# First feed-forward layer of a hybrid block: activations stationary in its first products, and the residual's affine part on VectorE

## The chip, the cores and the metric

The kernel runs on one core of one Trainium2 chip. The metric is device time in microseconds (us), the median of several executions. In the views, PE is TensorE (PEld its weight loads), DVE is VectorE, ACT is ScalarE, POOL is GpSimd and SP is SyncE, whose queue issues all the DMAs.

## What is computed

One block of a model on 256 tokens of width 2048, in fp32, batch 1: a feed-forward layer, a mixer (differential attention and a gated delta rule), and a second feed-forward layer, each with an affine modulation from a vector c and with a residual and a layer norm behind it.

```python
ada = (silu(c) @ w_ada + b_ada).reshape(B, 3, 3, D)
shift, scale, gate = ada[:, :, 0, None], ada[:, :, 1, None], ada[:, :, 2, None]
y = swiglu_ffn(x * (1.0 + scale[:, 0]) + shift[:, 0], w_ffn_in[0], w_ffn_out[0])
x = layer_norm(ALPHA * x + 0.5 * gate[:, 0] * y, ln_g[0], ln_b[0])
y = hybrid_mixer(x * (1.0 + scale[:, 1]) + shift[:, 1], ...)
x = layer_norm(ALPHA * x + gate[:, 1] * y, ln_g[1], ln_b[1])
y = swiglu_ffn(x * (1.0 + scale[:, 2]) + shift[:, 2], w_ffn_in[1], w_ffn_out[1])
x = layer_norm(ALPHA * x + 0.5 * gate[:, 2] * y, ln_g[2], ln_b[2])
```

`swiglu_ffn(h, w_in, w_out)` is `(silu(g) * u) @ w_out` with `g, u` the two halves of `h @ w_in`; each half is 5632 wide, 44 tiles of 128.

## The kernel before

**Products in three parts.** Every fp32 operand of a large product is split into a high half (`hi`, rounded to fp32r by ScalarE) and a low half (`lo`, the difference, by VectorE or GpSimd), and `mm3` makes a product of three matmuls: hi by hi, and the two mixed ones. There are two forms. With *weights stationary* (`_products`) a 128x128 piece of the weights stays in the array and 256 columns of the activations (all tokens) stream past it; the result has features on partitions. With *activations stationary* (`_xprod`, `_xstat`) a tile of 128 tokens stays and 512 columns of weights stream; the result has tokens on partitions, and to be the next layer's input it has to be turned by transposes (the `hT` tiles).

**The weight stream.** `k.plan` lists all weight chunks of 128 x 1024 (512 KB) in the order of use. `_dma` issues chunk `i` on SP's queue into one of 6 `raw` buffers, `_split` makes `hi` and `lo` of it in one of 4 pairs of buffers, and `weights()` hands a chunk to the products while up to three more are split ahead. `pool_lo` says who makes `lo`: GpSimd for every chunk (1), for every second one (2), or VectorE always (0).

**The order of work.** All engines run in order. The order is written by the program itself while it is built: the products are emitted in a straight line, with a planned clock `k.t` that they advance, and side jobs are generators ("threads") that `pump()` resumes between products when their planned time has come. `yield 8.0` in such a job means: not before 8 planned us from now. `bank()` hands out 4 PSUM banks in turn and `k.read` names the job that empties one.

**The first layer.** Its input h is made tile by tile (16 tiles of 128 features, `_first_h`): four chunks `sar` of w_ada per tile are loaded, VectorE reduces each to one column, then scales the tile of x (`hf`), ScalarE makes `h_hi` and GpSimd `h_lo`. Since h comes slowly, `start` visits the first 28 pairs of (gate, up) feature tiles several times, each time with the few tiles of h that are there. `VISITS` holds (first tile of h, number of tiles, pairs from, to), `START_LO` the `pool_lo` of each visit. A pair's bank holds gate and up side by side; it is copied to `acc` at the first visit (ScalarE) and added to it at the others (VectorE). At the last visit `_ffn_hid` adds, applies silu (ScalarE), multiplies and splits (VectorE, ScalarE). The products are named `mms`. The other 16 pairs of this layer, and the second feed-forward layer, are made by `_ffn_block`, activations stationary, four pairs (512 features) at a time: gate into two banks (two halves of the tokens), up into two more, silu, product, eight transposes, split. The second matrix's products (`_y_blocks`) follow, named `mx` as well.

**Side work beside it.** `_Ada` makes the gate rows on VectorE: chunks `ar` are multiplied and added into `acc<-ar,cs,acc`; at each quarter's end its sum is split (`acchi`, `acclo`) and two matmuls (`aps`) stand for it in PE's queue.

**The residual's affine part.** Behind a layer norm the kernel keeps x without ln_g and ln_b. For the mixer's and the second layer's residual, `_load_x` fetches x again, and then for each of four quarters loads a row of ln_g and of ln_b to all partitions (`rowg`, `rowb`, one buffer each) and has GpSimd multiply and add, four instructions of 128x512 a quarter.

**The layer norm.** `_Next.step(0)` sets `pool_lo` to 1 ahead of a layer's last output block, `rest` sets it back, so that GpSimd makes the low halves of the weights there.

Of the kernel before, what the change touches and what calls it, by code (L numbers as in the profile page):

```python
# [91 lines left out]
class _Kernel:  # L92
# [52 lines left out]
    def mm3(self, ps, lhs, rhs, start, stop):  # L145
        mm = self.nc.tensor.matmul
        mm(ps, lhsT=lhs[0], rhs=rhs[0], start=start, stop=False, skip_group_check=True)  # L147
        mm(ps, lhsT=lhs[0], rhs=rhs[1], start=False, stop=False, skip_group_check=True)  # L148
        mm(ps, lhsT=lhs[1], rhs=rhs[0], start=False, stop=stop, skip_group_check=True)  # L149
        self.t += 3 * _cols(ps) * 4.22e-4  # L150
# [136 lines left out]
def _xprod(k, ps, w, act, kt, j, t, lo, hi, last):  # L287
# [261 lines left out]
class _Next:  # L549
# [5 lines left out]
    def step(self, stage, ada, ln):  # L555
        k = self.k
        if stage == 0:
            k.pool_lo = 1
# [14 lines left out]
    def rest(self, ln):  # L573
# [20 lines left out]
        k.pool_lo = 0  # L594
# [81 lines left out]
def _load_x(k, a, pool, rows, tags, idx, delay, pace):  # L676
# [11 lines left out]
    for q in range(4 if idx is not None else 0):  # L688
# [56 lines left out]
def _ffn_hid(k, ps, hid, j, acc=None, back=1):  # L745

    hid.job(j, k.read(_ffn_hid_run(k, ps, hid, j, acc, hid.all[-1:]), back))


def _ffn_hid_run(k, ps, hid, j, acc, before):  # L750
    u = k.uid()
    g, up = ps[:, 0, :], ps[:, 1, :]
    if acc is not None:
        yield 0.2
        k.V.tensor_tensor(acc, acc, ps, ALU.add)
        g, up = acc[:, 0, :], acc[:, 1, :]
    yield 0.2
    while not all(th.done for th in before):
        yield 0.3
    sg = k.hp.tile([128, S], F32, tag="sg", name=f"sg{u}", bufs=2)  # L760
    k.A.activation(sg, g, AF.Silu)
    yield
    hf = k.hp.tile([128, S], F32, tag="hidf", name=f"hidf{u}", bufs=2)
    k.V.tensor_tensor(hf, sg, up, ALU.mult)
    yield
    both = k.hp.tile([128, 2, S], F32R, tag=f"hid{j}", name=f"hid{u}")
    hid[0][j], hid[1][j] = both[:, 0, :], both[:, 1, :]
    k.A.activation(hid[0][j], hf, AF.Copy)
    yield
    k.V.tensor_tensor(hid[1][j], hf, hid[0][j].bitcast(F32), ALU.subtract)  # L770


def _ffn_block(k, h, hid, b, before, pre):
# [5 lines left out]
    def gate(t, ps, lo, hi):  # L779
        yield 0.2  # L780
# [3 lines left out]
        k.A.activation(sg[t], ps, AF.Silu)  # L784

    def up(t, ps, lo, hi):
        yield 0.2
        k.V.tensor_tensor(sg[t], sg[t], ps, ALU.mult)
# [21 lines left out]
    if pre is None:  # L810
        _xstat(k, KT // 2, h, gate)
    else:
        for t in range(2):
            k.read(gate(t, pre[t], 0, 512), 2 - t)
    _xstat(k, KT // 2, h, up)
# [6 lines left out]
def _ffn(k, a, h, sub, items, interval, start, pre, finish, tail):  # L822
# [3 lines left out]
    with ExitStack() as fs:  # L826
        k.hp = hp = fs.enter_context(tc.tile_pool(name=f"hid{sub}", bufs=1))
        for half, size in enumerate(SIZES[sub]):
# [20 lines left out]
            turned = []  # L849
            for b in range(b0, size // 4):  # L850
                turned = [_ffn_block(k, h, hid, b, turned, None if b or half else pre)]
# [586 lines left out]
def _first_h(k, a, h, hp):  # L1438
# [18 lines left out]
    for i in range(SRAW):  # L1457
        load()
        if i == 3:
            loadx(0)  # L1460
    loadx(2)
    due = 0.0
    for i, (f, half, kind) in enumerate(plan):
# [11 lines left out]
        if i in FIRST_LOADS:  # L1475
            k._dma()
# [14 lines left out]
def tile_hybrid_block(ctx: ExitStack, tc: tile.TileContext, names, aps):  # L1491
# [83 lines left out]
    def start(h, hid, side):  # L1575

        with ExitStack() as st:
# [5 lines left out]
            accs = [k.hp.tile([128, 2, S], F32, tag=f"hid{j}", name=f"acc{j}") for j in range(hid.ready)]  # L1583
            k.pool_lo = 1
            for (kt0, n, ja, jb), lo in zip(VISITS, START_LO):
                h.need(k, kt0)
                k.pool_lo = lo
                npair, nchunk = max(1, 4 // n), max(1, n // 4)
                last = kt0 + n == KT
                for j0 in range(ja, jb, npair):  # L1590
                    pss = [k.bank([128, 2, S], "mms") for q in range(npair)]
                    for c in range(nchunk):
                        w = [x.rearrange("p (q r) -> p q r", q=npair) for x in k.weights()]
# [3 lines left out]
                    for q, ps in enumerate(pss):  # L1597
                        j = j0 + q
                        if last:
                            _ffn_hid(k, ps, hid, j, accs[j], npair - q)  # L1600
                        else:
                            k.read(add(accs[j], ps, kt0 == 0), npair - q)
                    if last and first is not None:
                        k.wait(lambda: first.done)
                        first = None
                        _ada_keep(k)
# [158 lines left out]
```

## Time and profile before

| | |
|---|---|
| three timed runs, us | 2392.42, 2392.65, 2395.93; median 2392.65 |
| profiled execution, us | 2389.68, span 2387.9 |
| mean granted TensorE clock | 0.984 |
| busy share of the span | PE 97%, PEld 87%, DVE 71%, ACT 43%, POOL 14% |
| moved by DMA | 581.70 MB, 244 GB/s on the mean |

Matmuls overlap, and a matmul's end is modelled; so how many start in a stretch says more than PE's busy time. The `x` count in a table of stretches is that number (a few records can be missing). In a row of the waits or of the timeline, the bracket holds the idle time ahead of the instruction and what ended it.

### The profile page before, as it was taken

How to read it: one execution, taken by the hardware profiler on the slowest of the kernel's cores; microseconds unless marked ns; L12 is line 12 of the kernel's file. 1: busy time of each engine (PE TensorE's matmuls, PEld its weight loads, DVE VectorE, ACT ScalarE, POOL GpSimd, SP SyncE). 2: the span in 40 equal slices, each digit the busy share in tenths (PEclk: the TensorE clock that was granted, in tenths of full speed). 3: DMA queues.
4: the chain of work that ended last, by engine and by line, in shares of the span. 5: the costliest groups of instructions: out<-in, count | busy, mean ns of one | idle time of the engine just before them, and what ended most of it. 6: DMA issues, size and time to landing. Idle time of an engine off the chain costs nothing.

```text
span 2387.9 us, 36796 instructions
## 1 busy us (share of the span) xinstructions
PE 2305.5 (97%) x14217; PEld 2071.9 (87%) x14217; DVE 1707.0 (71%) x2508; ACT 1033.1 (43%) x1390; POOL 329.1 (14%) x218
## 2 busy tenths in 40 slices
PE   6999999999999899999999999999999999999997
PEld 6999997888888889988999999987878888888886
DVE  5667888787775688878887887786787555544556
ACT  4434444434444444454444434444444443444432
POOL 5884000000001310000000220013050000000001
PEclk8999999999999999999999999999999999999999
DMA  9998878899875566454546888876888556655553
GB/s 362 332 327 292 300 250 274 305 339 322 315 267 189 176 204 209 157 173 149 170 162 244 298 296 306 286 282 204 310 302 309 189 192 194 193 187 192 188 187 111
DMA packets 166359, 581.70 MB, mean 244 GB/s; under 512 B 19820, under 2 KB 22812, under 8 KB 165416
## 3 DMA queue, kind: packets, MB, share of 16 engines
q1 hardware_dynamic: 166184, 579.36, 70.7%
q8 instruction: 111, 1.82, 0.3%
q14 instruction: 64, 0.52, 0.1%
HBM read 572.98 MB, written 7.88 MB: 243 GB/s over the span
## 4 chain that ended last, share of the span: by engine, by line
PE 86%; DVE 7%; issue 2%; DMA 1%; POOL 1%; ACT 1%; SPq 0%; DVEq 0%; ACTq 0%; POOLq 0%
PE mx L148 17%; PE mx L147 17%; PE mx L149 17%; PE mm L147 6%; PE mm L148 6%; PE mm L149 6%; PE mms L148 4%; PE mms L149 4%; PE mms L147 4%; DVE lo L88 2%; DVE acc L88 1%; PE UY L153 1%; DVE x L88 1%; ACT hi L88 1%; PE hT L158 1%
## 5 line engine op out<-in xcount | busy, mean ns | idle before, releaser
L88 ACT ACTIVATE hi<-raw 128x1024 fp32r<-128x1024 f32 x769 | 811.6, 1059 | 968.7 <-PE mx L149 669.3
L88 DVE TENSOR_TENSOR lo<-raw,hi 128x1024 fp32r<-128x1024 f32 x690 | 855.7, 1246 | 495.7 <-ACT hi L88 485.4
L147 PE MATMUL mx<-hi,h_hi 128*128 128x512 f32 x992 | 389.7, 393 | 0.0
L149 PE MATMUL mx<-hi,h_lo 128*128 128x512 f32 x992 | 387.2, 390 | 0.0
L148 PE MATMUL mx<-lo,h_hi 128*128 128x512 f32 x992 | 387.0, 390 | 0.0
L147 PE MATMUL mm<-h_hi,hi 128*128 128x256 f32 x1216 | 354.4, 291 | 0.0
L149 PE MATMUL mm<-h_hi,lo 128*128 128x256 f32 x1216 | 346.5, 285 | 3.4 <-DVE lo L88 3.4
L148 PE MATMUL mm<-h_lo,hi 128*128 128x256 f32 x1216 | 346.4, 285 | 0.0
L88 POOL TENSOR_TENSOR lo<-raw,hi 128x1024 fp32r<-128x1024 f32 x79 | 190.2, 2415 | 788.0 <-ACT hi L88 788.0
L147 PE MATMUL mx<-hi,hid 128*128 128x512 f32 (+1 forms) x768 | 285.1, 371 | 1.4 <-ACT hi L88 1.4
L148 PE MATMUL mx<-lo,hid 128*128 128x512 f32 (+1 forms) x768 | 284.7, 371 | 0.8 <-DVE lo L88 0.8
L149 PE MATMUL mx<-hi,hid 128*128 128x512 f32 (+1 forms) x768 | 284.5, 370 | 0.0
L147 PE MATMUL mms<-h_hi,hi 128*128 128x256 f32 x896 | 256.2, 286 | 10.2 <-ACT hi L88 5.9
L148 PE MATMUL mms<-h_lo,hi 128*128 128x256 f32 x896 | 256.2, 286 | 3.7 <-POOL h_lo L88 3.7
L149 PE MATMUL mms<-h_hi,lo 128*128 128x256 f32 x896 | 255.9, 286 | 1.6 <-POOL lo L88 1.6
L149 PEld LDWEIGHTS mm<-h_hi,lo 128*128 128x128 f32 x1216 | 235.2, 193 | 3.9 <-DVE lo L88 3.9
L147 PEld LDWEIGHTS mm<-h_hi,hi 128*128 128x128 f32 x1216 | 235.7, 194 | 1.7 <-issue 1.6
L148 PEld LDWEIGHTS mm<-h_lo,hi 128*128 128x128 f32 x1216 | 235.7, 194 | 0.7 <-issue 0.6
L149 PEld LDWEIGHTS mx<-hi,h_lo 128*128 128x128 f32 x992 | 186.6, 188 | 39.2
L147 PEld LDWEIGHTS mx<-hi,h_hi 128*128 128x128 f32 x992 | 186.7, 188 | 38.2 <-issue 0.2
L148 PEld LDWEIGHTS mx<-lo,h_hi 128*128 128x128 f32 x992 | 186.7, 188 | 38.0 <-issue 0.2
L147 PEld LDWEIGHTS mms<-h_hi,hi 128*128 128x128 f32 x896 | 174.4, 195 | 10.9 <-ACT hi L88 6.1
(304 smaller groups left out, 3236.2 us busy)
## 6 DMA issues: line engine op xcount, KB each, us to landing
raw<-in_w_ffn_in_dram SPq DMA_DIRECT2D x240, 512.0 KB, 4.7
raw<-in_w_ffn_out_dram SPq DMA_DIRECT2D x176, 512.0 KB, 4.1
raw<-in_w_first_dram SPq DMA_DIRECT2D x112, 512.0 KB, 5.0
ar<-in_w_gate_dram SPq DMA_DIRECT2D x96, 512.0 KB, 5.1
ar<-in_w_ada_dram SPq DMA_DIRECT2D x96, 512.0 KB, 5.1
sar<-in_w_ada_dram SPq DMA_DIRECT2D x64, 512.0 KB, 5.0
raw<-in_w_gab_dram SPq DMA_DIRECT2D x64, 512.0 KB, 4.5
raw<-in_w_kq_dram SPq DMA_DIRECT2D x32, 512.0 KB, 3.6
```

The source lines that it names most:

```text
L88: return f(*args, **kw)
L147: mm(ps, lhsT=lhs[0], rhs=rhs[0], start=start, stop=False, skip_group_check=True)
L148: mm(ps, lhsT=lhs[0], rhs=rhs[1], start=False, stop=False, skip_group_check=True)
L149: mm(ps, lhsT=lhs[1], rhs=rhs[0], start=False, stop=stop, skip_group_check=True)
L153: self.nc.tensor.matmul(ps, lhsT=lhsT, rhs=rhs, start=start, stop=stop, skip_group_check=True)
L158: self.nc.tensor.transpose(ps, src, self.ident if ident is None else ident)
```

## The change

1. The first layer's visits make blocks of four pairs with activations stationary. `VISITS` now counts blocks of four pairs: the first two visits take one tile of h each and two blocks; the third takes tiles 0 and 1 for the other five; the others have the old ranges. With one tile, one chunk holds gate and up of a block, in four banks. With more, `_xbanks` makes gate and then up, in two banks each. The last visit ends in the same `_ffn_block` as the other blocks, which adds `acc` first. `_ffn_hid` goes.
2. `mm3` gets an order; in `_xprod` the two matmuls with the high half of the weights come first.
3. At the start two chunks of `w_first` are issued behind the first x tile instead of behind the first two reductions. The first two chunks are split while `pool_lo` is still 0, so VectorE makes their low halves.
4. `_Next` no longer sets `pool_lo`.
5. The affine part's products and sums are VectorE's, one each 2 planned us, the first 6 behind the loads.

```diff
-VISITS = ((0, 2, 0, 28), (2, 2, 0, 28), (4, 4, 0, 28), (8, 4, 0, 12), (8, 8, 12, 28), (12, 4, 0, 12))
+VISITS = ((0, 1, 0, 2), (1, 1, 0, 2), (0, 2, 2, 7), (2, 2, 0, 7), (4, 4, 0, 7), (8, 4, 0, 3), (8, 8, 3, 7), (12, 4, 0, 3))
-FIRST_LOADS = (0, 1)
-START_LO = (1, 1, 1, 2, 0, 0)
+START_LO = (1, 1, 1, 1, 1, 2, 0, 0)
...
+    def mm3(self, ps, lhs, rhs, start, stop, order=((0, 0), (0, 1), (1, 0))):
+        for n, (i, j) in enumerate(order):
+            self.nc.tensor.matmul(ps, lhsT=lhs[i], rhs=rhs[j], start=start and n == 0, stop=stop and n == 2,
+                                  skip_group_check=True)
...
-          start=(kt == 0), stop=(kt == last))
+          start=(kt == first), stop=(kt == last), order=((0, 0), (1, 0), (0, 1)))
...
+def _xbanks(k, kt0, n, act, name="mx"):
+
+    pss = [k.bank([128, 512], name) for _ in range(2)]
+    for c in range(n // 2):
+        w = k.weights()
+        for j in range(2):
+            for t in range(2):
+                _xprod(k, pss[t], w, act, kt0 + 2 * c + j, j, t, 0, 512, kt0 + n - 1, kt0)
+    return pss
...
         if stage == 0:
-            k.pool_lo = 1
...
         ln.norm(1, 0)
-        k.pool_lo = 0
...
-        yield 8.0
+        yield 4.0
         for t in range(2):
-            k.P.tensor_tensor(x[t][:, sl], x[t][:, sl], g, ALU.mult)
-            k.P.tensor_tensor(x[t][:, sl], x[t][:, sl], b, ALU.add)
+            for v, op in ((g, ALU.mult), (b, ALU.add)):
+                yield 2.0
+                k.V.tensor_tensor(x[t][:, sl], x[t][:, sl], v, op)
...
+    def summed(i, t, ps):
+        if accs is None:
+            return ps
+        acc = accs[4 * b + 2 * i + t]
+        k.V.tensor_tensor(acc, acc, ps, ALU.add)
+        return acc
...
+    for i in range(2):
+        k._dma()
     loadx(2)
...
-        if i in FIRST_LOADS:
-            k._dma()
...
+                if n == 1:
+                    for b in range(ba, bb):
+                        w = k.weights()
+                        pss = [k.bank([128, 512], "mms") for _ in range(4)]
                         for q, ps in enumerate(pss):
-                            _products(k, ps, [x[:, q, :] for x in w], kt0 + 4 * c, n // nchunk, [h, h], c == 0,
-                                      c == nchunk - 1)
+                            _xprod(k, ps, w, h, kt0, q // 2, q % 2, 0, 512, kt0, kt0)
+                        for q, ps in enumerate(pss):
+                            k.read(add(accs[4 * b + q], ps, kt0 == 0), 4 - q)
+                    continue
+                for b in range(ba, bb):
+                    if kt0 + n < KT:
+                        for i in range(2):
+                            for t, ps in enumerate(_xbanks(k, kt0, n, h, "mms")):
+                                k.read(add(accs[4 * b + 2 * i + t], ps, kt0 == 0), 2 - t)
+                        continue
...
+                    _ffn_block(k, hid, b, hid.all[-1:], banks, accs)
```

The order on PE at its first products, before (`mms` are banks, `h_hi`, `h_lo` the halves of h, `hi`, `lo` those of a weight chunk):

```order
L147 MATMUL mms_199<-h_hi_91,hi_187 128x256
L148 MATMUL mms_199<-h_lo_92,hi_187 128x256
L149 MATMUL mms_199<-h_hi_91,lo_188 128x256
L147 MATMUL mms_199<-h_hi_91,hi_187 128x256
L148 MATMUL mms_199<-h_lo_92,hi_187 128x256
```

and now, at the same place:

```order
L146 MATMUL mms_211<-hi_187,h_hi_91 128x512
L146 MATMUL mms_211<-hi_187,h_lo_92 128x512
L146 MATMUL mms_211<-lo_188,h_hi_91 128x512
L146 MATMUL mms_212<-hi_187,h_hi_91 128x512
L146 MATMUL mms_212<-hi_187,h_lo_92 128x512
```

What streams and what stays have changed places, a matmul is twice as wide, and the weights' low half comes last.

The order on PE in the last visit's first block, now (`hT` are the banks of the transposes of the block made before it, `sg` its products on VectorE):

```order
L146 MATMUL mms_2756<-hi_2691,h_hi_91 128x512
L146 MATMUL mms_2756<-hi_2691,h_lo_92 128x512
L146 MATMUL mms_2756<-lo_2692,h_hi_91 128x512
L156 MATMUL hT_2777<-ident,sg_2640 128x128
L156 MATMUL hT_2777<-ident,sg_2643 128x128
L156 MATMUL hT_2777<-ident,sg_2640 128x128
L156 MATMUL hT_2777<-ident,sg_2643 128x128
L146 MATMUL mms_2755<-hi_2711,h_hi_91 128x512
```

Before, no transposes stand in this part of PE's queue; now two groups of four stand there for each block.

The order on VectorE at the mixer's first quarter of the affine part, now (`x` two halves of the tokens, `lo` a chunk's low half, `acc<-ar` a gate step):

```order
L87 TENSOR_TENSOR x_12568<-x_12568,rowg_12987 128x512
L87 TENSOR_TENSOR lo_13103<-raw_12904,hi_13102 128x1024
L87 TENSOR_TENSOR x_12568<-x_12568,rowb_12988 128x512
L87 TENSOR_TENSOR x_12569<-x_12569,rowg_12987 128x512
L87 TENSOR_TENSOR lo_13138<-raw_12937,hi_13137 128x1024
L87 TENSOR_TENSOR x_12569<-x_12569,rowb_12988 128x512
L87 SCALAR_TENSOR_TENSOR acc_12870<-ar_13023,cs,acc_12870 128x512 x2
```

Before, the four lines with `rowg` and `rowb` stand on GpSimd, and the others follow each other on VectorE.

## Rows read from the trace of the kernel before

**Rows 1.** The page: busy time with share of the span, and the chain's shares.
```profile
PE 2305.5 (97%) x14217; PEld 2071.9 (87%) x14217; DVE 1707.0 (71%) x2508; ACT 1033.1 (43%) x1390; POOL 329.1 (14%) x218
...
PE 86%; DVE 7%; issue 2%; DMA 1%; POOL 1%; ACT 1%; SPq 0%; DVEq 0%; ACTq 0%; POOLq 0%
```
**Rows 2.** Stretches for one tile: length, busy (x instructions) by engine, clock, DMA (`mms`, `mx`).
```profile
60.00:120.00 60.00, 60.00 (x502) 59.97 (x501) 20.77 (x31) 4.27 (x8) 1.00 0.92 333
...
480.00:540.00 60.00, 60.00 (x266) 49.67 (x266) 2.74 (x4) 0.00 (x0) 1.00 0.92 332
```
**Rows 3.** Timeline of PE, transposes in the first layer's other blocks: start, length, instruction.
```profile
570.06 0.60 PE L158 MATMUL hT<-ident,sg 128*128 128x128 f32 x4
...
570.73 0.40 PE L148 MATMUL mx<-lo,h_hi 128*128 128x512 f32 x1
```
**Rows 4.** Timeline of the start, and a stretch (PE, PEld, DVE, ACT, POOL).
```profile
12.75 0.42 ACT L88 ACTIVATE h_hi<-hf 128x256 fp32r<-128x256 f32 x1 [10.19 <-DVE hf L88]
...
14.54 1.06 ACT L88 ACTIVATE hi<-raw 128x1024 fp32r<-128x1024 f32 x1 [1.37 <-DMA raw<-in_w_first_dram]
...
15.65 0.58 PE L147 MATMUL mms<-h_hi,hi 128*128 128x256 f32 x1 [5.91 <-ACT hi L88]
...
27.45 0.58 PE L148 MATMUL mms<-h_lo,hi 128*128 128x256 f32 x1 [3.25 <-POOL h_lo L88]
...
10.00:40.00 30.00, 15.15 (x93) 14.27 (x94) 18.67 (x28) 11.33 (x16) 16.76 (x9) 0.66 1.02 404
```
**Rows 5.** Two stretches at the first layer's end, and PE's timeline.
```profile
330.00:350.00 20.00, 15.59 (x106) 14.79 (x105) 17.56 (x28) 7.91 (x14) 0.00 (x0) 0.83 0.69 220
360.00:390.00 30.00, 25.99 (x114) 20.29 (x114) 25.84 (x36) 15.04 (x23) 0.00 (x0) 1.00 0.82 273
...
336.35 0.79 PE L153 MATMUL aps<-acchi,ones 128*128 128x512 f32 x1 [3.46 <-ACT acchi L88]
338.09 0.79 PE L153 MATMUL aps<-acclo,ones 128*128 128x512 f32 x1 [0.95 <-DVE acclo L88]
```
**Rows 6.** Groups of VectorE, 0 to 400 us: count, busy us, mean ns, idle before.
```profile
L88 DVE TENSOR_TENSOR lo<-raw,hi 128x1024 fp32r<-128x1024 f32 x62 | 76.6, 1236 | 35.2 <-ACT hi L88 35.1
L88 DVE TENSOR_TENSOR acc<-acc,mms 128x512 f32<-128x512 f32 x96 | 64.7, 682 | 36.2 <-PE mms L149 30.6 <-ACT acc L88 5.6
...
L88 DVE SCALAR_TENSOR_TENSOR acc<-ar,cs,acc 128x512 f32<-128x512 f32 x52 | 38.9, 749 | 1.0
...
L88 DVE TENSOR_TENSOR hidf<-sg,acc 128x256 f32<-128x256 f32 x28 | 11.7, 418 | 0.0
```
**Rows 7.** The affine part: timeline of VectorE and PE, stretches, landing of `rowg`.
```profile
1749.41 3.48 DVE L88 SCALAR_TENSOR_TENSOR acc<-ar,cs,acc 128x512 f32<-128x512 f32 x2
...
1380.72 0.79 PE L153 MATMUL aps<-acchi,ones 128*128 128x512 f32 x1 [3.03 <-ACT acchi L88]
...
1370.00:1390.00 20.00, 16.69 (x112) 15.89 (x111) 18.86 (x15) 7.00 (x9) 14.38 (x8) 0.83 0.87 295
...
1750.00:1770.00 20.00, 17.80 (x78) 14.20 (x77) 19.19 (x15) 8.55 (x11) 13.21 (x8) 1.00 0.82 270
...
DMA to landing us min/median/max: 4.7/4.7/4.7
```
**Rows 8.** Timeline of GpSimd and VectorE at the first layer norm.
```profile
782.27 2.39 POOL L88 TENSOR_TENSOR lo<-raw,hi 128x1024 fp32r<-128x1024 f32 x1 [0.48 <-ACT hi L88]
...
782.52 0.42 DVE L88 SCALAR_TENSOR_TENSOR res<-mx,gate 128x256 f32<-128x256 f32 x1 [13.59 <-PE mx L149]
782.98 1.97 DVE L88 TENSOR_TENSOR x<-x,res 128x256 f32<-128x256 f32 x1
```
**Rows 9.** Stretches of all engines: the last two columns are DMA share and GB/s.
```profile
60.00:120.00 60.00, 60.00 (x502) 59.97 (x501) 42.38 (x63) 27.41 (x33) 52.67 (x26) 1.00 0.92 333
...
40.00:50.00 10.00, 10.00 (x85) 10.00 (x85) 5.85 (x10) 6.91 (x11) 9.11 (x5) 1.00 1.02 409
```
**Rows 10.** The transposes' tile `hT`: idle time ahead of it until VectorE's product.
```profile
  DVE sg L88: 0.3, 1
```

More of the change, by code (lines that the diff above doesn't have):

```diff
@@ L284, in _tile, with _xprod @@
     return part[kt] if isinstance(part, dict) else part[:, kt, :]
-def _xprod(k, ps, w, act, kt, j, t, lo, hi, last):
+def _xprod(k, ps, w, act, kt, j, t, lo, hi, last, first=0):
     act.need(k, kt)
@@ L740, in _y_blocks, with _ffn_block, gate @@
         return finish.step(3, ada, ln)
[L745 to L753, printed above, removed]
-        yield 0.2
[L755 to L773, printed above, removed]
-    sg = {}
-    def gate(t, ps, lo, hi):
-        yield 0.2
+def _ffn_block(k, hid, b, before, banks, accs=None):
+    sg = {}
+    def summed(i, t, ps):
[4 more added lines that the diff above has]
+        return acc
+    def gate(t, ps):
+        yield 0.2
+        src = summed(0, t, ps)
         while not all(th.done for th in before):
@@ L783, in gate, with up @@
         sg[t] = k.hp.tile([128, 512], F32, tag=f"sg{t}", name=f"sg{k.uid()}")
-        k.A.activation(sg[t], ps, AF.Silu)
-    def up(t, ps, lo, hi):
+        k.A.activation(sg[t], src, AF.Silu)
+    def up(t, ps):
         yield 0.2
-        k.V.tensor_tensor(sg[t], sg[t], ps, ALU.mult)
+        src = summed(1, t, ps)
+        while t not in sg:
+            yield 0.3
+        k.V.tensor_tensor(sg[t], sg[t], src, ALU.mult)
     def turn(ups):
@@ L808, in turn @@
                 k.V.tensor_tensor(hid[1][j], ps[:, q, :], hid[0][j].bitcast(F32), ALU.subtract)
[L810 to L815, printed above, removed]
+    for i, done in enumerate((gate, up)):
+        for t, ps in enumerate(banks(i)):
+            k.read(done(t, ps), 2 - t)
     th = k.spawn(turn(list(k.users[-2:])))
@@ L848, in _ffn, with banks @@
                     ada = side()
-            turned = []
+            turned = hid.all[-1:]
             for b in range(b0, size // 4):
-                turned = [_ffn_block(k, h, hid, b, turned, None if b or half else pre)]
+                def banks(i, b=b):
+                    return pre if pre and b == half == i == 0 else _xbanks(k, 0, KT, h)
+                turned = [_ffn_block(k, hid, b, turned, banks)]
             res = _y_blocks(k, size // 2, hid, ada, sub, half == 0, ln if half else None, finish, tail)
@@ L1582, in start @@
             first.step()
-            accs = [k.hp.tile([128, 2, S], F32, tag=f"hid{j}", name=f"acc{j}") for j in range(hid.ready)]
-            k.pool_lo = 1
-            for (kt0, n, ja, jb), lo in zip(VISITS, START_LO):
+            accs = [k.hp.tile([128, 2, S], F32, tag=f"hid{j}", name=f"acc{j}").rearrange("p a b -> p (a b)")
+                    for j in range(hid.ready)]
+            for (kt0, n, ba, bb), lo in zip(VISITS, START_LO):
                 h.need(k, kt0)
                 k.pool_lo = lo
[L1588 to L1593, printed above, removed]
-                        for q, ps in enumerate(pss):
-                            _products(k, ps, [x[:, q, :] for x in w], kt0 + 4 * c, n // nchunk, [h, h], c == 0,
-                                      c == nchunk - 1)
[L1597 to L1606, printed above, removed]
-                        st.close()
-                        ada = side()
@@ new lines, in start, with banks @@
+                if n == 1:
+                    for b in range(ba, bb):
+                        w = k.weights()
+                        pss = [k.bank([128, 512], "mms") for _ in range(4)]
+                        for q, ps in enumerate(pss):
+                            _xprod(k, ps, w, h, kt0, q // 2, q % 2, 0, 512, kt0, kt0)
[8 more added lines that the diff above has]
+                        continue
+                    def banks(i):
+                        nonlocal first, ada
+                        pss = _xbanks(k, kt0, n, h, "mms")
+                        if first is not None:
+                            k.wait(lambda: first.done)
+                            first = None
+                            _ada_keep(k)
+                            st.close()
+                            ada = side()
+                        return pss
+                    _ffn_block(k, hid, b, hid.all[-1:], banks, accs)
```

19 lines of the change are left out of this document (9 added, 10 removed).

## The prediction

> **What bounds the kernel now.** I read the page first, for which engine the end hangs on, then one table of stretches per stage, then the waits at the places that the edit touches. TensorE is busy 97% of the span, and the chain that ended last runs through it for 86% [rows 1]. Its busy time is modelled, so I cost matmuls by their spacing: how many start in a stretch in which nothing else runs on PE. In the first layer, where weights are stationary and 256 columns of h stream, 502 start in 60 us, 119.5 ns apart; where activations are stationary and 512 columns of weights stream, 266 start, 225.6 ns apart [rows 2]. So the kernel is a queue of matmuls, and an edit pays if it makes the spacing smaller per column, or fills a hole in that queue. There are four sorts of hole near the edit: the start, the end of the first layer, the two places where GpSimd makes the residual's affine part, and the two layer norms. The profiled execution took 2389.68 us (span 2387.9); the median of the three timed runs is 2392.65, 3.0 above it. I work out a difference from the profiled one and take it off the median.
>
> **First layer, the matmuls.** 2688 matmuls of 256 columns go, 1344 of 512 come. Per pair that is 2 x 119.5 - 225.6 = 13.4 ns, in all 18.0 us less. Both forms run elsewhere in this kernel at the spacings used, so the bounds are narrow: 17 to 19.
>
> The new form leaves tokens on partitions, so each of the 7 blocks needs 8 transposes more, in 14 groups of four. In the second feed-forward layer four of them and the matmul behind them take from 570.06 to 570.73, 0.67 us, where a matmul alone takes 0.23 [rows 3]: 0.44 us a group, 6.2 us in all. Net: **-11.8 us**.
>
> The Trainium skill ("TensorE: Matmul & The Clock Gate", section "Back-to-back issue gap") speaks against this: its isolated gap is N/2.4 + 2.5 ns, that is 109 ns for 256 columns and 216 for 512. By that a pair gains 2.5 ns, 3.4 us in all, and the transposes would eat it: +2.8 instead of -11.8. The rows of this kernel show 119.5 where the rule has 109, so I take the rows.
>
> **The start.** Before, PE first multiplies at 15.65, when a first weight chunk has landed (ScalarE starts its split at 14.54 upon the DMA) although h's first tile was split by 13.2; it then needs the second tile of h after six matmuls, and starts to run through only at 27.45 [rows 4]. From 10 to 40 us it starts 93 matmuls, which at full spacing are 11 us of work. Now the first two chunks are issued ahead of the second x tile, their low halves go to VectorE, and the first two visits need one tile of h each. ScalarE can split chunk 0 right behind h's first tile: 13.2 + 1.1 gives 14.3 for PE's start, with 24 matmuls of 512 columns to do before the second tile, which I leave at 24 to 27 us. The clock is granted at the low level there (0.66 on the mean of 10 to 40, between 1.2 and 2.4 GHz), so I estimate twice the spacing, 0.45 us, for the first twelve: to about 20. Then PE waits: ScalarE has the split of the fifth chunk ahead of the four copies that free the banks (1.1 + 0.6 us). With another such gap behind chunk 1 and full clock from about 31, PE reaches some 76 matmuls of 512 by 40 us, where it had the equal of 46.5: 29.5 x 0.2256 = 6.7. I take **-6 us**; between 2 (low clock until 36) and 11 (one short gap).
>
> **The end of the first layer.** In 330 to 350 PE starts 104 matmuls and two for a gate [rows 5]: at full spacing 12.9 us of 20, so 7.1 us are lost, 4.4 in the two waits of the gate's matmuls for ScalarE and VectorE and the rest at the low clock behind them (granted 0.83). In 360 to 390, 114 at 225.6 ns are 25.7 of 30: 4.3 lost. Cause: VectorE. In the last visit's 13 chunks it has, by the kernel's order, 14 splits of 1.24, 13 sums of 0.68, 16 gate steps of 0.75 and 21 hidden-tile steps of 0.42 [rows 6]: 47 us, where PE has 13 x 24 x 0.1195 = 37.3. After, with 512-wide products, there are 12 sums, 6 products of about 0.68 and 8 subtractions beside the same splits and gate steps: 44.9, against 35.2 + 2.6 us of PE. VectorE is still the late one, by 7 instead of 10 us. Of the 11.4 us lost I expect somewhat over half to stay: **-5 us**, between 0 and -11. This also says that part of the matmul gain is given back here unless VectorE keeps up, which is why I stay at the low side.
>
> **The affine part.** Thirty-two GpSimd instructions go. While they run, a pair of VectorE gate steps takes 3.48 us instead of 1.5 (2 x 0.75), so VectorE falls behind and PE waits 3.03 us for a gate's split [rows 6, 7]. In 1370 to 1390 PE starts 110 matmuls and two for the gate: 6.4 us of 20 lost, at granted 0.83; in 1750 to 1770, 76 of 225.6 ns: 2.4 lost. In all 8.8. VectorE now does 32 of about 0.68 us, 22 us spread over two stretches of some 60, less than the slowdown that goes. Each now stands in VectorE's queue in front of splits, and waits there if its row of ln_g or ln_b hasn't landed: that takes 4.7 us from issue [rows 7], while between the last addition of a quarter and the next product VectorE has some six to seven us of other work in the order. So I hide it under that. I take **-6 us**, between 0 and -10. The sums are done later, but the first residual that needs them is over 100 us away.
>
> **The layer norms.** At two stage ends the low halves move from GpSimd to VectorE, which is idle for 13 us ahead of the first. There GpSimd's split from 782.27 holds the 256-wide addition of 782.98 for 1.97 us, where the product of the same width ahead of it takes 0.42 [rows 8]. A 1.24 us split on VectorE will stand in front instead: about 0.85 less, twice: **-1.7 us**, bounds 0 and -3. The new order inside a triple (weights' low half last) has one answer: PE hardly waits for low halves in that form, 0.
>
> **Sum:** -11.8 - 6 - 5 - 6 - 1.7 = -30.5; 2389.7 becomes 2359.2, and the median 2392.65 becomes **2362**.
>
> **Rivals.**
> *The transfers hold the first layer.* It moved 333 GB/s from 60 to 120 us; PE 1.059 times as fast wants 353. For it: VectorE and GpSimd already wait on loads at times. Against it: 409 GB/s flowed from 40 to 50 us [rows 9]. If 333 is the most, the first 68 of 112 chunks gain nothing, 10.9 us are lost, 2373. The skill ("SBUF — State Buffer", section "A bandwidth-pool intuition that's wrong (but worth ruling out)") puts HBM's share of a core at about 358 GB/s, which would leave this rival no slack; the 409 GB/s of the row is above it.
> *The affine part blocks VectorE.* If the rows land late, that term is 0 and the sum is -24.5, 2368.
> *Columns alone count.* If one 512-column matmul costs two spacings of 119.5 here, the term is +6.2 and the result 2380. Against it: the two rows of [rows 2].
> *Slower: the transposes wait in PE's queue.* PE works in order, and a block's first transposes stand between matmuls at a place the planner chose; VectorE runs behind plan at the end of this layer. If PE waits there as it did for the gate at 336, each costs 7.1 us with the clock behind it. Without the end term the gain is 25.5, so from four of seven blocks on the kernel is slower, and with all seven it is 2392.65 - 25.5 + 49.7 = 2417. Against it: over the 120 transposes of before, waits for VectorE's product come to 0.3 us [rows 10].
>
> **How the numbers follow.** Forecast 0.70; transfers 0.12; affine 0.07; columns 0.03; all faster, 0.92. Slower 0.05. Small effects that cancel each other, 0.03. A measurement of this kernel tells about 0.2% (4.8 us) from no change. The forecast's best bounds sum to -46 (2347), its worst to -14 (2379); the first three rivals lie inside or at that edge, so the range is 2349 to 2379.
>
> **What would show it.** Spacing near 225.6 ns in the first layer's middle, and DMA above 345 GB/s there (else the transfers' rival). PE's first product near 14.3 and some 150 half-size equivalents by 40 us. Waits at the gate's matmuls near the layer's end under 3 us, and none over 2 us at the first layer's transposes. No VectorE instruction of twice its length near 1350 to 1390 and 1740 to 1785, and VectorE's waits for ln_g and ln_b short. Wrong would be a first layer that ends less than 15 us earlier, or new PE holes in the mixer, whose order the planner shifts a little.

## The result, and the profile after

The changed kernel took 2357.76 us, the median of four runs (2357.18 to 2359.76); the kernel before took 2392.94 beside it. The ratio is 0.9852, with a 95% interval of 0.9835 to 0.9869, so 31 to 39 us were gained. The forecast was 2362 in a range of 2349 to 2379. A second measurement (`after_again`, below) gave 2357.6 and 0.9846 [0.9833, 0.9859].

The page of the changed kernel, busy time and the chain's shares, as in [rows 1]:

```profile
PE 2289.3 (97%) x12929; PEld 2002.5 (85%) x12929; DVE 1710.3 (73%) x2550; ACT 1030.7 (44%) x1376; POOL 230.5 (10%) x170
...
PE 89%; DVE 5%; DMA 1%; issue 1%; ACT 1%; POOL 1%; SPq 0%; DVEq 0%; ACTq 0%; POOLq 0%
```

TensorE bounds the kernel still, with 1288 records fewer. VectorE's share of the chain has gone from 7% to 5%. The gain's place is read from landmarks: the first start of a tile that both kernels have (and, for the gates, their last product), taken from the tile's own list. All times in us from the start of the span.

| landmark | before | after | difference |
|---|---|---|---|
| last product named `mms` | 360.7 | 340.9 | -19.8 |
| first transpose of the first layer norm (`lnt`) | 789.5 | 767.1 | -22.4 |
| first product of the mixer (`pre`) | 793.4 | 770.7 | -22.7 |
| first tanh of the mixer's last stage (`gth`, ScalarE) | 1281.7 | 1261.3 | -20.4 |
| last product with a gate there (`gth`, VectorE) | 1536.9 | 1508.1 | -28.8 |
| last transpose of the second layer norm | 1642.2 | 1612.8 | -29.4 |
| end of the span | 2387.9 | 2355.4 | -32.5 |

So the first layer gave 22 us; the mixer lost 2 ahead of its last stage and gained 8 in the stage with the affine part; the second layer gave 3. The profiled execution of before lies 3 below its median, which is why the medians differ by 35 and the spans by 32.5.

Stretches of the first layer's middle in the changed kernel (length, then busy time and instructions of PE, PEld, DVE, ACT and POOL, granted clock, DMA share, GB/s); they answer [rows 2] and [rows 9]:

```profile
60.00:120.00 60.00, 59.69 (x262) 48.88 (x261) 46.84 (x69) 27.31 (x33) 54.82 (x27) 1.00 0.95 361
120.00:180.00 60.00, 60.00 (x266) 49.69 (x266) 40.30 (x62) 24.85 (x27) 56.23 (x28) 1.00 0.95 352
```

266 in 60 us are 225.6 ns, the spacing forecast, and 361 GB/s is more than the 353 that the rival of the transfers said would be needed and not be had. It is also above the 358 GB/s that the Trainium skill ("SBUF — State Buffer", section "A bandwidth-pool intuition that's wrong (but worth ruling out)") gives as a core's share of HBM. The Trainium skill gets that share by dividing a stack's rate between two cores; only one core runs here, so the row shows that the share was no limit of this kernel, and no run here tests the share itself.

The start, timelines of ScalarE and of PE (start, length, instruction, in the bracket the idle time ahead of it and what ended it), and one stretch; they answer [rows 4]:

```profile
13.43 2.11 ACT L87 ACTIVATE hi<-raw 128x1024 fp32r<-128x1024 f32 x2
21.56 1.06 ACT L87 ACTIVATE hi<-raw 128x1024 fp32r<-128x1024 f32 x1 [6.02 <-DMA raw<-in_w_first_dram]
22.84 1.06 ACT L87 ACTIVATE hi<-raw 128x1024 fp32r<-128x1024 f32 x1 [0.22 <-DMA raw<-in_w_first_dram]
24.20 1.06 ACT L87 ACTIVATE hi<-raw 128x1024 fp32r<-128x1024 f32 x1 [0.31 <-DMA raw<-in_w_first_dram]
25.17 2.04 ACT L87 ACTIVATE acc<-mms 128x512 f32<-128x512 f32 x4
```
```profile
14.52 0.79 PE L146 MATMUL mms<-hi,h_hi 128*128 128x512 f32 x1 [4.95 <-ACT hi L87]
25.80 0.80 PE L146 MATMUL mms<-hi,h_hi 128*128 128x512 f32 x1 [6.17 <-ACT acc L87]
31.66 0.50 PE L146 MATMUL mms<-hi,h_hi 128*128 128x512 f32 x1 [1.45 <-ACT acc L87]
```
```profile
10.00:40.00 30.00, 17.82 (x60) 13.09 (x61) 20.36 (x31) 12.96 (x18) 14.84 (x8) 0.77 1.01 396
```

PE begins at 14.5, as forecast, and makes the first chunk's 12 products by about 19.6. Then it stands for 6.17 us. The four copies that free its banks are ready to run, but on ScalarE three splits stand ahead of them, and the first of these waits 6.02 us for its chunk. By 40 us 60 products of 512 have started, not 76.

The end of the first layer, to be held against [rows 5]: stretches, and PE's waits from 200 to 400 us (total, times, longest).

```profile
300.00:330.00 30.00, 28.22 (x133) 23.03 (x132) 28.72 (x40) 15.96 (x25) 0.00 (x0) 1.00 0.77 256
330.00:350.00 20.00, 19.22 (x89) 15.53 (x88) 19.86 (x31) 8.87 (x13) 0.00 (x0) 1.00 0.80 260
350.00:380.00 30.00, 29.27 (x128) 22.80 (x128) 24.50 (x30) 14.02 (x17) 0.00 (x0) 1.00 0.88 298
```
```profile
PE aps L151 <- DVE acclo L87: 1.8, 1, 1.8
PE hT L156 <- DVE sg L87: 0.8, 2, 0.6
PE mx L146 <- DVE hid L87: 0.7, 2, 0.5
```

The three stretches lose 1.78 + 0.78 + 0.73 = 3.3 us, and the granted clock stays at 1.00, where 11.4 were lost before. VectorE is busy 19.86 of 20 us there all the same.

The affine part, to be held against [rows 7]: one stretch, and VectorE's timeline at the first row of the second layer.

```profile
1370.00:1390.00 20.00, 19.88 (x166) 19.68 (x165) 16.58 (x23) 7.88 (x9) 0.00 (x0) 1.00 0.85 286
```
```profile
1749.43 0.69 DVE L87 TENSOR_TENSOR x<-x,rowg 128x512 f32<-128x512 f32 x1 [2.77 <-DMA rowg<-in_ln_g_dram]
1750.04 1.22 DVE L87 TENSOR_TENSOR lo<-raw,hi 128x1024 fp32r<-128x1024 f32 x1
1751.18 0.69 DVE L87 TENSOR_TENSOR x<-x,rowb 128x512 f32<-128x512 f32 x1
1751.78 1.53 DVE L87 SCALAR_TENSOR_TENSOR acc<-ar,cs,acc 128x512 f32<-128x512 f32 x2
```

166 products and a full clock stand where there were 112 at 0.83, a pair of gate steps takes 1.53 us again, and a wait of 2.77 us for a row stops VectorE without a hole on PE.

The first layer norm on VectorE, against [rows 8]:

```profile
760.51 1.23 DVE L87 TENSOR_TENSOR lo<-raw,hi 128x1024 fp32r<-128x1024 f32 x1 [1.65 <-ACT hi L87]
761.65 0.42 DVE L87 SCALAR_TENSOR_TENSOR res<-mx,gate 128x256 f32<-128x256 f32 x1
762.11 0.42 DVE L87 TENSOR_TENSOR x<-x,res 128x256 f32<-128x256 f32 x1
```

The addition takes 0.42 us instead of 1.97, with the split in front of it, as forecast.

### The profile page after: what moved, and what is told of

The parts are those of the page before. It is cut to its first block, busy times and chain, and to the rows that moved or that the text cites. A ratio compares the mean times of both kernels' runs of the same rounds, so it can differ in the third digit from the quotient of the medians.

```text
span 2355.4 us, 34160 instructions
## 1 busy us (share of the span) xinstructions
PE 2289.3 (97%) x12929; PEld 2002.5 (85%) x12929; DVE 1710.3 (73%) x2550; ACT 1030.7 (44%) x1376; POOL 230.5 (10%) x170
## 4 chain that ended last, share of the span: by engine, by line
PE 89%; DVE 5%; DMA 1%; issue 1%; ACT 1%; POOL 1%; SPq 0%; DVEq 0%; ACTq 0%; POOLq 0%
PE mx L146 52%; PE mm L146 18%; PE mms L146 13%; PE pre L146 2%; DVE lo L87 1%; PE hT L156 1%; PE UY L151 1%; DVE x L87 1%; ACT hi L87 1%; PE Y L151 0%; POOL h_lo L87 0%; POOL pol L87 0%; DMA ar<-in_w_gate_dram 0%; DMA raw<-in_w_gab_dram 0%; PE av L151 0%
## 5 line engine op out<-in xcount | busy, mean ns | idle before, releaser
L146 PE MATMUL mx<-hi,hid 128*128 128x512 f32 (+1 forms) x1536 | 440.0, 371 | 0.7 <-DVE hid L87 0.7
L146 PEld LDWEIGHTS mx<-hi,hid 128*128 128x128 f32 x1536 | 279.2, 189 | 51.2 <-DVE hid L87 1.6
L146 PE MATMUL mms<-hi,h_hi 128*128 128x512 f32 x448 | 177.6, 396 | 12.6 <-ACT acc L87 7.6
L146 PE MATMUL mms<-hi,h_lo 128*128 128x512 f32 x448 | 175.8, 392 | 0.3 <-POOL h_lo L87 0.3
L146 PE MATMUL mms<-lo,h_hi 128*128 128x512 f32 x448 | 175.7, 392 | 0.0
L146 PEld LDWEIGHTS mx<-lo,hid 128*128 128x128 f32 x768 | 144.8, 188 | 24.6
L87 POOL TENSOR_TENSOR lo<-raw,hi 128x1024 fp32r<-128x1024 f32 x63 | 151.6, 2418 | 29.3 <-ACT hi L87 29.2
```

The lines of the kernel that those rows point to most:

```text
L87: return f(*args, **kw)
L146: self.nc.tensor.matmul(ps, lhsT=lhs[i], rhs=rhs[j], start=start and n == 0, stop=stop and n == 2, skip_group_check=True)
```

## The experiments

The kernel before moved between 2391 and 2395 us from one set of runs to the next, so kernels of different sets are compared by their ratios to it; 0.001 is 2.4 us. The changed kernel stands at 0.9846 to 0.9852.

### The parts one by one

Three kernels take parts of the change back, one makes a part alone. `a_pool` gives the affine part back to GpSimd:

```diff
-        yield 4.0
+        yield 8.0
...
-            for v, op in ((g, ALU.mult), (b, ALU.add)):
-                yield 2.0
-                k.V.tensor_tensor(x[t][:, sl], x[t][:, sl], v, op)
+            k.P.tensor_tensor(x[t][:, sl], x[t][:, sl], g, ALU.mult)
+            k.P.tensor_tensor(x[t][:, sl], x[t][:, sl], b, ALU.add)
```

> The changed kernel with the affine part alone back on GpSimd. Theory: the landmarks of the two traces give the affine part 8.1 us in the mixer and 2.9 in the second layer, so 2358 + 11 = 2369, with pairs of gate steps near 3.5 us instead of 1.53 and holes on TensorE at the same two places as in the kernel before. Rival, the prediction's size: +6, 2364. Rival: the gain there came from the shifted order and not from GpSimd: within 2 of 2358.

Measured: 2370.21 us, ratio 0.9902 [0.9887, 0.9917]; 12 to 13 us slower than the changed kernel. VectorE's timeline in it, and its stretches there:

```profile
1352.46 2.44 DVE L87 SCALAR_TENSOR_TENSOR acc<-ar,cs,acc 128x512 f32<-128x512 f32 x2
1354.82 4.54 DVE L87 TENSOR_TENSOR lo<-raw,hi 128x1024 fp32r<-128x1024 f32 x2
1359.29 1.52 DVE L87 SCALAR_TENSOR_TENSOR acc<-ar,cs,acc 128x512 f32<-128x512 f32 x2
```
```profile
1350.00:1370.00 20.00, 17.42 (x130) 16.81 (x129) 19.41 (x15) 7.57 (x10) 11.85 (x8) 0.91 0.79 274
1370.00:1390.00 20.00, 19.40 (x161) 19.20 (x161) 17.07 (x22) 6.57 (x8) 0.00 (x0) 1.00 0.87 309
1390.00:1410.00 20.00, 18.65 (x151) 18.10 (x151) 17.85 (x22) 9.03 (x12) 0.00 (x0) 1.00 0.86 300
```

A pair of splits takes 4.54 us instead of 2.4, and PE stands in three stretches in a row, the last two after GpSimd is done (POOL 0.00). Those two look like VectorE catching up, but that is not shown: it sat idle for 1.64 us ahead of 1381.89, waiting for a gate chunk, and `a_noaff` below has such waits too.

`b_aff` is the kernel before with the reverse of that edit.

> The kernel before with the affine part alone moved to VectorE. Theory: -11, 2382, with the mixer's part (between the first tanh of its last stage and the first product of its output) 8 us shorter and the second layer's 3. Rival, the prediction's size: -6, 2387. Rival: the affine part gains only in the order that the changed first layer leaves behind: 0 to -3.

Measured: 2381.49, ratio 0.9947 [0.9935, 0.9960]: -12.7 us. From the first tanh to the last product with a gate it takes 246.4 us. All ten profiles with these sums on VectorE (two of them of the changed kernel) take 246.3 to 247.2 there, the three with them on GpSimd 253.7 to 255.2. The part is worth the same in either kernel, about twice what was forecast.

`a_noaff` leaves the 32 products and sums out of the changed kernel, so the residuals of the mixer and the second layer lack ln_g and ln_b:

```diff
-            for v, op in ((g, ALU.mult), (b, ALU.add)):
+            for v in (g, b):
                 yield 2.0
-                k.V.tensor_tensor(x[t][:, sl], x[t][:, sl], v, op)
+                k.chain += 0.74
```

> The changed kernel with the affine part's 32 products and sums left out (the rows are still loaded). Theory: VectorE makes them in time that it has to spare, so the total stays within 2 of 2358; all that the move could give is taken. Rival: they, or the 2.8 us wait for a row, still delay gate steps and splits: 3 us or more below 2358.

Measured: 2359.87, ratio 0.9864 [0.9848, 0.9879]. Without 22 us of VectorE's work the kernel is no faster. It is 2 to 4 us slower: the order of 144 of PE's instructions moved between 1300 and 1500 us, the mixer's last stage took 249.4 us instead of 246.8, and two waits of PE at the gate came back:

```profile
PE aps L151 <- ACT acchi L87: 0.8, 1, 0.8
PE aps L151 <- DVE acclo L87: 0.6, 1, 0.6
```

In the mixer, then, the moved order could hide a small cost of the sums. Around the second layer's rows, from 1700 to 1850 us, PE waits for VectorE in neither kernel, and from the last product with a gate to the end of the span it took 846.7 us against 847.3: 0.6 less is all that shows there. The two waits also stand here without any affine work, GpSimd's or VectorE's; so those of 0.77 and 0.57 us behind GpSimd's last instruction in `a_pool` may come from the place of the gate's matmuls in the order.

`a_small` takes back the layer norms' low halves and the order inside a triple:

```diff
+            k.pool_lo = 1
...
+        k.pool_lo = 0
...
-          start=(kt == first), stop=(kt == last), order=((0, 0), (1, 0), (0, 1)))
+          start=(kt == first), stop=(kt == last))
```

> The changed kernel with GpSimd's low halves back at the two layer norms and the old order inside a triple in _xprod. Theory: +1.7 from the norms (0.85 each, to be seen as a 256-wide addition of about 2 us instead of 0.42 at each norm's start) and 0 from the order: 2359.5. Rival: the order of a triple matters wherever VectorE's low half is late, in the first layer's last visit most: +4 or more, with waits of TensorE for lo between 300 and 390 us.

Measured: 2359.89, ratio 0.9857 [0.9843, 0.9870]; 1 to 3 us, as expected, too little to be told from nothing. The addition takes 1.97 us again in its timeline, and PE waits once in the first layer for `lo`, 0.5 us.

`a_form` takes back the affine part and these small edits together; only the first layer is left.

> The changed kernel with the affine part back on GpSimd, GpSimd's low halves back at the layer norms and the old order inside a triple in _xprod: only the first layer's new form and the start are left of the change. Theory from the two traces' landmarks: the first layer is worth 22 us by the first product of the layer norm's transposes, so 2393 - 22 = 2371 and the gain is whole before 790 us. The prediction's three terms for it (11.8 + 6 + 5) give 2370, so the total can't tell them apart; the places can: by the theory about 60 matmuls start from 10 to 40 us and no hole of over 2 us lies between 300 and 390. Rival: the new order of a triple or the norms' low halves made part of that gain; then this kernel ends 4 us or more above 2371.

Measured: 2374.2, ratio 0.9908 [0.9894, 0.9922]: -22.0 us, between 19 and 25. Its first layer norm starts at 768.1, against 767.1 with the whole change and 789.5 before, and from 10 to 40 us 62 products start. The largest loss in ten us between 300 and 390 is 2.0 (busy 7.99 from 320 to 330). The three measured parts, 22.0 of the first layer, 12 to 13 of the affine part and 1 to 3 of the small edits, make the whole within their intervals.

### The end of the first layer

`a_dve` makes six low halves of the last visit twice:

```diff
+        if self.twice and i % 2 == 0:
+            self.nc.vector.tensor_tensor(lo, raw, hi.bitcast(F32), ALU.subtract)
...
+                k.twice = kt0 == 12
```

> The changed kernel with every second low half of the last visit's 12 chunks made twice on VectorE: 6 instructions of 1.22, 7.3 us more, nothing else moved. First theory: VectorE's total work in that stretch made the hole at the end of the first layer (47 us before, 44.9 after, busy 49 of 50 us from 300 to 350 in the changed kernel); then TensorE waits there again, with the clock's fall behind it: +4 to +9, 2362 to 2367. Rival: it was the chain of small steps per pair, which crosses between VectorE and ScalarE four times and is gone now; then three chunks split ahead (8.7 us of products) cover the 7.3 and the total stays within 2 of 2358.

Measured: 2364.24, ratio 0.9879 [0.9863, 0.9895], 6.5 us by the medians. Two stretches of it:

```profile
320.00:330.00 10.00, 5.96 (x17) 4.32 (x16) 9.82 (x14) 3.67 (x6) 0.00 (x0) 0.66 0.57 197
350.00:360.00 10.00, 7.43 (x29) 5.56 (x28) 9.93 (x16) 2.67 (x4) 0.00 (x0) 0.86 0.81 262
```

At the same gate matmuls (1.6 us for `acchi`, 2.4 for `acclo`) and the transposes behind (2.4), PE stands again, and the granted clock of the ten us falls to 0.66. PE's, ScalarE's and GpSimd's instructions stand in the same order as in the changed kernel. So 7.3 us of work on VectorE alone bring back a hole like that of the kernel before, and the rival, that three chunks split ahead would cover them, falls. Whether the chain of small steps had a share in the hole of before is not shown.

`a_gate7` goes the other way: `GATE_PACE = 7.0` instead of 6.0.

> The changed kernel with the gate's steps in the first layer planned 7 us apart and not 6 (GATE_PACE). VectorE then has some 1.4 us less to do in the last visit, since a step more falls behind it. Theory: VectorE's work in that stretch is what TensorE still waits for there (1.8 us at the gate's low half near 321, 0.7 near 355); with less of it -1 to -3, 2355 to 2357. Rival: the waits hang on the place where the planner puts the gate's matmuls, and these move to another place that is as bad: within 1 of 2357.7, or above.

Measured: 2352.44 (2348.95 to 2357.49), ratio 0.9836 [0.9822, 0.9849], 2 to 4 us better than the changed kernel by the ratios, 5 by the medians. The intervals overlap: it has the lowest median here, but its lead is not settled. Its PE from 200 to 400 us, and the same stretch as above:

```profile
PE mx L146 <- DVE hid L87: 0.7, 1, 0.7
PE aps L151 <- DVE acclo L87: 0.3, 1, 0.3
```
```profile
320.00:330.00 10.00, 10.00 (x49) 8.27 (x49) 9.93 (x16) 6.20 (x10) 0.00 (x0) 1.00 0.80 271
```

The wait of 1.8 is 0.3, and the first layer norm starts at 763.5, 3.6 us earlier. The edit also moves the gate's matmuls in PE's order, as its rival said, so it agrees with `a_dve` but could not decide alone.

### The transposes

`a_tr2` issues every transpose of the first layer's seven blocks twice:

```diff
-                    k.tr(ps[:, q, t * 128:(t + 1) * 128], sg[t][:, f * 128:(f + 1) * 128])
+                    for _ in range(2 if accs else 1):
+                        k.nc.tensor.transpose(ps[:, q, t * 128:(t + 1) * 128], sg[t][:, f * 128:(f + 1) * 128], k.ident)
...
```

> The changed kernel with each transpose of the first layer's seven blocks issued twice (56 more, in 14 groups of four). Theory: they cost TensorE's queue 0.44 us a group, +6.2, 2364. Rival: they cost what a 512-wide matmul's place costs only where they wait; with nothing waiting, well under half: +0 to +3.

Measured: 2361.71, ratio 0.9873 [0.9855, 0.9890]; +4.0 by the medians, +5 to 6 by the ratios. The first layer norm starts 4.1 later. Where PE would have stood for VectorE, the added ones fit into the hole (from 320 to 330 it is busy 9.05 us instead of 8.22). Ahead of 300 us, where PE waits for nothing, the first six groups put its products back by 2.5 us together, 0.41 each; so the 0.44 of the forecast is right where PE is the late one.

`a_tight` lets PE come to them too early:

```diff
-        yield max(0.0, k.V.t - k.t) + 2.0
+        yield 0.0 if accs else max(0.0, k.V.t - k.t) + 2.0
```

> The changed kernel with the first layer's transposes put into TensorE's queue as soon as the block's last product is, 3 and 12 matmuls behind it, and not some ten us later by plan. It makes the prediction's slower rival real. That rival priced a wait at 7.1 us, the clock's fall included: seven blocks, +20 to +50, 2378 to 2408. Rival: waits of one to two us each with no fall of the granted clock, +7 to +14, 2365 to 2372; then the rival was priced too high.

Measured: 2382.67, ratio 0.9951 [0.9939, 0.9963], +25 us. PE's waits from 200 to 400 us:

```profile
PE hT L156 <- DVE sg L87: 18.5, 14, 2.8
```

Fourteen waits, 1.3 us on the mean; with what the clock adds (0.83 to 0.94 in several stretches) 25 / 7 = 3.6 us a block.

### The start

`a_start` puts the first visit's copies ahead of the later splits:

```diff
-                        w = k.weights()
                         pss = [k.bank([128, 512], "mms") for _ in range(4)]
+                        w = k.weights(0 if kt0 else WB - 2)
```

> The changed kernel, in which the first visit takes its four banks ahead of its chunk and lets only one further chunk be split ahead, so that ScalarE's copies of a bank stand ahead of the splits of the third to fifth chunk. Theory: the hole of 6.17 us from 19.6 to 25.8 is ScalarE waiting 6.02 us for the third chunk's transfer with the copies queued behind; with the copies ahead TensorE goes on at about 20, makes the second chunk's 12 matmuls and then waits for h's second tile (split by 22.1): some 80 matmuls by 40 us instead of 60, -4 to -5 us, 2353. Rival: TensorE is then held by the transfers of chunks and of w_ada (404 GB/s there), which don't come any earlier: new waits for DMA behind 30 us and a total within 2 of 2358.

Measured: 2356.51, ratio 0.9850 [0.9832, 0.9868]: no gain that can be told. The mechanism of the hole is right, the gain isn't kept. Stretches of it, and of the changed kernel (second fence):

```profile
10.00:40.00 30.00, 21.27 (x72) 15.94 (x73) 23.32 (x37) 15.49 (x22) 15.96 (x9) 0.83 1.03 405
...
90.00:120.00 30.00, 27.76 (x114) 22.26 (x113) 23.33 (x35) 11.26 (x13) 23.72 (x13) 0.94 0.89 325
```
```profile
90.00:120.00 30.00, 29.69 (x130) 24.06 (x129) 24.93 (x37) 11.97 (x14) 27.00 (x14) 1.00 0.91 340
```

PE starts 12 products more by 40 us and 16 fewer from 90 to 120. It then waits for h's eighth tile. This is the row of that wait:

```profile
107.39 0.51 PE L146 MATMUL mms<-hi,h_lo 128*128 128x512 f32 x1 [2.00 <-POOL h_lo L87]
```

GpSimd makes that low half behind five splits of 2.4 us. `a_hlo` has the same edit and gives that low half to VectorE:

```diff
-    k.P.tensor_tensor(h[1][:, f, :], hf, h[0][:, f, :].bitcast(F32), ALU.subtract)
+    (k.V if first else k.P).tensor_tensor(h[1][:, f, :], hf, h[0][:, f, :].bitcast(F32), ALU.subtract)
...
```

> The changed kernel with the first visit's copies ahead of the splits (as in the run before, which reached 75 matmuls by 40 us instead of 60 but had lost them by 120 us) and with the low halves of the first layer's h tiles on VectorE instead of GpSimd. Theory: the gain was given back near 107 us, where the eighth tile's low half stood on GpSimd behind five splits of 2.4 us; with it on VectorE TensorE no longer waits there nor at 25.7 (1.8 us): 3 to 5 us kept, 2353 to 2355. Rival: h comes no earlier in any case, since its 64 chunks of w_ada come at the rate of the transfers and VectorE is late itself: the wait moves to the high half or to VectorE, and the total stays within 1.5 of 2356.5.

Measured: 2358.73, ratio 0.9848 [0.9835, 0.9861]. The rival was right on the place: the wait moved, and by the ratio the kernel is where `a_start` was (0.9850). Its number, within 1.5 of 2356.5, was missed by the median. Timelines of PE and VectorE:

```profile
109.09 0.50 PE L146 MATMUL mms<-hi,h_hi 128*128 128x512 f32 x1 [2.65 <-ACT h_hi L87]
```
```profile
96.30 2.34 DVE L87 TENSOR_TENSOR h_lo<-hf,h_hi 128x256 fp32r<-128x256 f32 x1 [0.49 <-ACT h_hi L87]
...
107.07 1.52 DVE L87 TENSOR_SCALAR hf<-xt,ab 128x256 f32<-128x256 f32 x1
```

The wait is now for the high half, since VectorE makes `hf` of that tile at 107.07, 3.2 us later than in `a_start` (103.87). One of the new low halves took 2.34 us beside GpSimd where one alone takes 0.43. VectorE makes h, the sums and now the low halves, and it is the late one.

### The stretch without an edit

`after_again` is the changed kernel unchanged.

> The changed kernel once more, as the base of this comparison. From the first product of the mixer (770.7) to its first tanh (1261.3) the changed kernel took 490.6 us, the kernel before 488.3, and the kernels in which nothing there is changed 486.0 to 491.8. Theory: this stretch varies from one execution to the next, and the 2 us that the changed kernel lost there are no effect of the change: median within 2 of 2357.8, and the stretch anywhere from 486 to 492. Rival: the shifted order costs 2 us there each time: again 490 to 491.

Measured: 2357.6 (2354.68 to 2358.74), ratio 0.9846 [0.9833, 0.9859]. The mixer's stretch took 490.6 us again, as its rival had it. But that rival's cause, a shifted order, is out: from the first `pre` to the last `UY` of the mixer the instructions of PE, VectorE, ScalarE and GpSimd stand in the same order in the kernel before and after, but for the two low products inside 64 triples, which the change swaps; and `a_small`, with the old order inside the triples, took 489.0. `a_dve`, whose order differs from the changed kernel's only by its six added instructions, all ahead of 347 us, took 486.0; `a_gate7` took 493.8. So the 2 us are within what this stretch varies by from kernel to kernel. That it varies from one execution to the next, as the theory had it, is not shown: the two of the changed kernel agree. What sets it within these 8 us stays open.

## Why the prediction was right, step by step

**First layer, the matmuls: right.** The spacing is 225.6 ns, so the 18.0 stand; the transposes' 6.2 measured 4 to 6. Of the 22.4 us of the first layer, 3.0 came at the start and 8.1 at its end, as follows below; 11.3 are left for this part, where 11.8 were forecast. The rival of the isolated gaps, with +2.8 for this part, falls by that and by `a_form`: some 22 us came from the first layer with its start alone. Its formula (the Trainium skill, "TensorE: Matmul & The Clock Gate", section "Back-to-back issue gap") is that of a single, isolated matmul; this is a stream, in which 119.5 and 225.6 ns were measured.

**The start: right mechanism, half the size.** PE's first product came at 14.5 (14.3 forecast). The step that failed is the gap behind the first chunk: I put the copies behind one split of 1.1 us, the fifth chunk's, and three stood there, the first of them held 6.02 us by its transfer. 60 products instead of 76 started by 40 us: (60 - 46.5) x 0.2256 = 3.0 us, not 6. `a_start` shows besides that a larger gain at the start would have been given back by 120 us.

**The end of the first layer: right direction, too careful.** 3.3 us are lost instead of 11.4; -8 against -5 forecast. The term that failed is "somewhat over half to stay", for a lateness of 7 instead of 10 us: some 30% stayed. In the second profile of the changed kernel (second fence) the same wait of 1.8 us took the clock with it, and 33 products started instead of 41:

```profile
320.00:330.00 10.00, 8.22 (x41) 6.48 (x40) 8.93 (x13) 6.12 (x11) 0.00 (x0) 1.00 0.72 230
340.00:350.00 10.00, 9.22 (x43) 7.30 (x42) 9.93 (x17) 4.77 (x7) 0.00 (x0) 1.00 0.90 281
```
```profile
320.00:330.00 10.00, 8.21 (x33) 6.51 (x32) 8.84 (x14) 4.81 (x10) 0.00 (x0) 0.83 0.74 247
340.00:350.00 10.00, 10.00 (x49) 8.27 (x48) 9.93 (x16) 4.96 (x8) 0.00 (x0) 1.00 0.93 286
```

It cost nothing by the end: from 340 to 350, where PE waits for VectorE's `sg` in the first profile, it didn't in the second, and the first layer norms start at 767.1 and 767.0. VectorE is busy 9.93 of these 10 us in both, so it sets the pace there, and what PE lost to the clock it would have waited. `a_dve` shows that VectorE's work can make the hole; `a_gate7` agrees.

**The affine part: the term that was mis-sized most.** -6 was taken, 11 by the landmarks and 12 to 13 by the runs came. I had read 8.8 us in two stretches and cut them for VectorE's own instructions and for rows that land late. Neither shows a cost: `a_noaff` is no faster, and VectorE's waits of up to 2.77 us for a row reach PE nowhere. And I stopped reading at 1390, with the last GpSimd instruction; the kernel before still loses 1.25 us behind it:

```profile
1401.00:1421.00 20.00, 18.75 (x152) 18.18 (x151) 17.70 (x23) 7.93 (x10) 0.00 (x0) 1.00 0.89 319
```

`a_pool` shows the same tail; whether it is VectorE's lateness or the place of the gate's matmuls stays open.

**Layer norms and the order in a triple: right**, 1 to 3 us together against 1.7.

**The rivals.** *Transfers*: out, 361 GB/s. *The affine part blocks VectorE*: out. *Columns alone*: out. *Slower by the transposes' waits*: in the changed kernel they come to 0.8 us; `a_tight` makes the case real and prices it at 3.6 us a block, half of the 7.1 of the forecast, which had put the gate's long wait of before in its place. Even with all seven blocks the kernel stayed 12 us faster than before, so the rival made real did not turn the sign.

The sum came out 4 to 6 us short of the gain, with 3 too much at the start, 3 too little at the layer's end, 5 to 7 too little for the affine part, and nothing for the 2 us that the mixer lost ahead of its last stage. That the total lies within 5 us of the forecast is in part luck, since these errors cancel in part.

## What to carry to other kernels

Where a helper engine slows its neighbour, taking over the work can be cheaper than sharing; read the holes behind the last slow instruction, too. Where another engine sets the pace, a hole or a lower clock on the one that waits can cost nothing, so follow a loss to the next common landmark before it is counted. A gain at the start of a pipeline is worth only what the next producer lets through; look for the engine that makes the input, not only for the one that waits. And an in-order queue that holds both loads' consumers and bank releases should have the releases first, though a closed hole must still be shown to be kept.

## What the runs showed of the hardware

GpSimd beside VectorE stretches some of VectorE's instructions far more than others. Splits and gate steps, which read two tiles from SBUF, took up to about twice their length (1.22 to 2.3 us, 0.75 to 1.78), and `h_lo` in `a_hlo` went from 0.43 to 2.34; the 104 sums of the first layer that read one operand from PSUM took 671 to 690 ns, though GpSimd was busy for over 90% of the time from 60 to 180 us. The Trainium skill ("SBUF — State Buffer", section "Who interferes with whom") says that a VectorE instruction with two inputs in SBUF contends with a GpSimd instruction that reads SBUF, and that one with at most one SBUF input does not, outside the two-port modes; these rows agree. The scaling of `hf` reads one tile and took 0.41 us alone and up to 1.53 beside GpSimd, so one input is not always safe; no row tells whether it ran in such a mode.

A row of ln_g took 4.7 us from issue to landing before, 6.0 in the changed kernel and 6.7 in `b_aff`, with the same bytes. And a wait of PE of 1.8 us at the same place left the granted clock at 1.00 in one execution of the changed kernel, while it was 0.83 over those ten us in another.
